# A hybrid decoder layer on one core: TensorE's order pinned slot by slot

## The chip, the cores and the metric

The kernel runs on one core of a Trainium2 chip. The metric is the device time of one execution in microseconds; lower is better. The median of the three runs shown of the kernel before is 1281.58 us.

## The reference, cut to what matters

One layer of a hybrid trunk for a prompt of 2048 positions and, beside it, 8 sequences of 4 new positions each, all with 1024 channels. `h = rmsnorm(x)` goes through one projection of 25 blocks of 128 columns. 13 of these blocks are shifted in time and feed an RWKV-7 recurrence of 8 heads of 64; 4 are its gate; 4 feed causal means over windows of 2, 4, 8 and 16 positions, and 4 are the gate of these.

```python
def _wkv_step(S, inp):
    r, w, k, v, kk, a = inp
    sa = jnp.einsum('bhvk,bhk->bhv', S, -kk)
    S = S * w[:, :, None, :] + sa[..., None] * (kk * a)[:, :, None, :] + v[..., None] * k[:, :, None, :]
    y = jnp.einsum('bhvk,bhk->bhv', S, r)
    return S, y
...
    out = jnp.concatenate([o_rwkv, o_pool], axis=-1) @ w_out.astype(f32)
    return x.astype(f32) + out, p_rwkv[:, -1], S_fin, u_ext[:, -POOL_BUF:]
```

The recurrence's output is normed per head, gated and joined with the gated means; an output projection of 1024 x 1024 and a last RMSNorm follow. The states after the last position are outputs too.

## The kernel before, in words

**Main work.** The prompt is cut into 4 groups of 512 positions. Every group has 25 projections (`proj`, L330): 8 chunks of 128 input channels, each with three products into one PSUM bank (L345 to L347: high part of the weights with the high and the low part of `x`, low part with the high). One such chunk is called a **slot** here. After each slot the generator yields, so a group has 200 slots and the four groups 800 (in the last group, which carries the 32 new positions too, a slot is two chunks of 272 columns). The output projection (`out_tile`, L1143) follows: 16 tiles of 16 slots each. While `x` of the first group arrives, `first_x` and `first_norm` (L238, L266) make its norm afterwards; for later groups `stats` and `prep_x` (L218, L280) prepare it in lane `x`.

**Side work.** Per group there are 4 head pairs, called **units** (`unit`, L522), each 48 slots long: the projections of r, k, window input, v and the two gates. When the projection of k has ended, VectorE and ScalarE shift it and make from it the blocks `abd` and `bk` and, for the key norms, a high and a low part `h_sq` and `l_sq` (L536 to L550, L471 to L475). The unit's recurrence is then done in chunks of 64 positions by side work:

- `decay` (L483): two products of the low-rank part of the block m = 12 (`lora_in` L378, `lora_out` L391), before the unit.
- `key_norms` (L502): the products `sq` and `bo` (L479, L480). The row `dS` goes to DRAM by ScalarE's queue (L513).
- `products` (L575): four steps of `pa` (L588), then, once the fold before has ended (`pend`), four steps of `pb` (L619).
- `solve` (L628): the blocks `Ab` go to DRAM by ScalarE's queue (`dA`, L637) and come back as `L` on SyncE's queue (L642). GpSimd then runs a substitution of 31 double operations (L654, L656) and three masks (L666, L668) as soon as `pb` is done. TensorE transposes its result (`xt`, L676) and does `q1` and `q2` (L695, L703).
- `fold` (L728): four times `z` (L733), copied into a block matrix by ScalarE and VectorE, and `f` (L741), added to `F` by VectorE.
- `pair_chain` (L763): eight dependent steps `ch` (L774), VectorE making the next state between them. `pair_back` (L803) norms the output in some 20 small VectorE operations and transposes it (`try`, L811).
- `values` and `pool_out` (L713, L859): one block of transposes `trv`, and one product `po`.

**What sets the order.** `run` (L461) calls `side()` after every slot; `side()` steps each lane's generator once. A number of `yield`s is a delay in slots. The compiler's list scheduler then orders every engine's instructions by priority and by when it thinks that they are ready. `tc.issue_after(ins)` adds an order edge: what the block traces on `ins`'s engine stands behind `ins` in the queue, without waiting for it to finish. In `side()` that instruction is the slot's last product (`mark[0]`). So a side product can't stand ahead of its slot, but can stand any number of slots behind it; and nothing holds the main products back. A unit starts only if fewer than two units are alive and lane `prod` is empty; until then it calls `side()` without main products.

Of the kernel before, what the change touches and what calls it, by code (L numbers as in the profile page):

```python
# [2 lines left out]

# [13 lines left out]
P = 128  # L17
# [43 lines left out]
def tile_trunk(ctx, tc, xT, xtok, xsT, xstok, par, w_in, wlora, pool_w, w_out, norm_f, st_shift, st_wkv, st_pool,  # L61
# [268 lines left out]
    def proj(g, m, xs):  # L330

        i = order.index((g, m))
        hi, lo = wts.pop(i)
        late_load = i + 2 < len(order) and order[i + 2][0]
        if not late_load:
            w_load(i + 2)
        last = g == NG - 1
        segs = []
        w = 272 if last else 512
        for s in range(2 if last else 1):  # L340
            pp = bank("pp", f"pp_{g}_{m}_{s}", 3) if i else bank("ch", "pp_first", 1)
            c = slice(s * w, (s + 1) * w)
            for kc in range(KC):
                xh, xl = xs[kc]
                PE.matmul(pp[:, :w], hi[:, kc, :], xh[:, c], start=(kc == 0), stop=False)  # L345
                PE.matmul(pp[:, :w], hi[:, kc, :], xl[:, c], start=False, stop=False)  # L346
                mark[0] = PE.matmul(pp[:, :w], lo[:, kc, :], xh[:, c], start=False, stop=(kc == KC - 1)).ins  # L347
                if s == 0 and kc == 2:
                    w_split(i + 1)
                    if late_load:  # L350
                        w_load(i + 2)
                if not last or kc % 2:
                    yield
            if g == 0 and m != 12:
                V.tensor_tensor(out=pp, in0=pp, in1=rb0[0], op=mult)
            if last:
                A.activation(spr[:, m, 16 * s:16 * s + 16], pp[:, 256:272], AF.Copy)
                segs.append((pp, 256 * s, 256))
            else:
                segs.append((pp, 0, G))  # L360
        return segs
# [44 lines left out]
            V.scalar_tensor_tensor(out=sg[:, a:a + n], in0=t1[:, a:a + n], scalar=1.0, in1=pp[:, :n], op0=add, op1=mult)  # L406
        return sg

    DH, DZ, DP, YQ = 6, 2, 4, 16

    def c3(ap):
        return ap.rearrange("p (c t) -> p c t", t=CH)
# [3 lines left out]
    rb0, low = [], []  # L416
    pend = [0]
    made = [None]
    chb = []
    lanes = {"prod": [], "solve": [], "fold": [], "chain": [], "x": [], "tail": []}  # L420
    late = []
# [23 lines left out]
    def drain(lane):  # L445
        while lanes[lane]:
            step(lane)

    def side():
        if not mark:  # L450
            return
        with tc.issue_after(mark[0]):
            step("solve")

            with tc.high_priority(0):
                step_late()
                step("prod")
                step("fold")
                step("chain")
# [42 lines left out]
    def key_norms(g, j, u, kk2, prod):  # L502

        nm = f"{g}_{j}"
        a = head_sums(kk2, f"sq_{nm}")
        for _ in range(DH + 2):
            yield
        sq = head_sums_mm(a, f"sq_{nm}")
        sqs = sb.tile([P, 512], F32, tag="tmp", name=f"sqs_{nm}", bufs=3)
        A.activation(sqs, sq, AF.Copy)  # L510
        for h in range(2):
            for b in range(2):
                nc.scalar.dma_start(u["dS"][b, h:h + 1],  # L513
                                    sqs[64 * h:64 * h + 1].rearrange("p (c b t) -> p b c t", b=2, t=32)[:, b])
        a = head_sums(prod, f"bo_{nm}")
        for _ in range(DH):
            yield
        bo = head_sums_mm(a, f"bo_{nm}")
        u["bv"] = sb.tile([P, 512], F32, tag="bv", name=f"bv_{nm}")
        A.activation(u["bv"], bo, AF.Copy)  # L520

    def unit(g, j, xs, nxs, lst, nst):  # L522
        nm = f"{g}_{j}"
        u = {}
        later((DZ if g else DZ + 7) if j == 0 else 1, decay(g, j, lst, u))
        r = shift(g, j, (yield from proj(g, j, xs)), "rps", 1)
        k = shift(g, 4 + j, (yield from proj(g, 4 + j, xs)), "kps", 1)
        while alive[0] >= 2 or lanes["prod"]:
            side()
        alive[0] += 1  # L530
        lam, cs, tha = u["lam"], u["cs"], u["tha"]
        kk2 = sb.tile([P, 512], F32, tag="tmp", name=f"kk2_{nm}", bufs=3)
        A.activation(kk2, k, AF.Square, scale=pr[:, KK + j:KK + j + 1])
        for h in range(2):
            q = slice(64 * h, 64 * h + 64)
            V.scalar_tensor_tensor(out=abd[q, :, q], in0=c3(k)[q], scalar=pr[q, KK + j:KK + j + 1],  # L536
                                   in1=lam[q, :, 0:CH], op0=mult, op1=mult)
        ab = sb.tile([P, 512], F32, tag="t1", name=f"ab_{nm}")
        A.activation(ab, tha, AF.Identity, scale=nkk[:, j:j + 1], bias=nkk[:, j:j + 1])
        V.tensor_tensor(out=cs, in0=k, in1=cs, op=mult)  # L540
        V.tensor_tensor(out=bk[:, :, 0:CH], in0=c3(cs), in1=c3(ab), op=mult)
        rd = sb.tile([P, NCH, CH], F32, tag="rd", name=f"rd_{nm}", bufs=1)
        V.tensor_tensor(out=rd, in0=c3(r), in1=lam[:, :, 1:], op=mult)
        A.activation(tha, tha, AF.Identity, scale=hka[:, j:j + 1], bias=oka[:, j:j + 1])
        V.tensor_tensor(out=bk[:, :, CH:2 * CH], in0=c3(cs), in1=c3(tha), op=mult)  # L545
        for h in range(2):
            q = slice(64 * h, 64 * h + 64)
            nc.sync.dma_start(rbd[q, :, h], rd[q])
        prod = sb.tile([P, 512], F32, tag="pd", name=f"prod_{nm}", bufs=1)
        V.scalar_tensor_tensor(out=c3(prod), in0=rd, scalar=pr[:, RK + j:RK + j + 1],  # L550
                               in1=bk[:, :, CH:2 * CH], op0=mult, op1=mult)
        dS = dr.tile([2, 2, NCH, 32], F32, tag="dS", name=f"dS_{nm}")
        u.update(rd=rd, dS=dS)
        lanes["prod"].append(products(g, j, u))
        kn = key_norms(g, j, u, kk2, prod)
        next(kn)
        late.append(kn)
        for m in SEQ[2:]:
            if m == 17:
                d = yield from pool_in(g, j, xs)  # L560
            elif m == 8:
                u["v"] = shift(g, 8 + j, (yield from proj(g, 8 + j, xs)), "kps", 1)
                later(8, values(g, j, u))
            elif m == 21:
                sg = gate(g, 21 + j, (yield from proj(g, 21 + j, xs)), "th0")
                later(DP, pool_out(g, j, d, sg))
            else:
                u["sg"] = gate(g, 13 + j, (yield from proj(g, 13 + j, xs)), "sg")
            if m == (SEQ[3] if SEQ[2] == 8 else 8):
                V.tensor_tensor(out=u["bv"], in0=u["bv"], in1=u["v"], op=mult)  # L570
            if m == SEQ[4] and j == NPAIR - 1 and g < NG - 1:
                drain("x")
                lanes["x"].append(prep_x(g + 1, nst, nxs, range(XB - KC, KC)))

    def products(g, j, u):  # L575

        nm = f"{g}_{j}"
        for _ in range(3):
            yield

        ka = sb.tile([P, NCH, P], F32, tag="ka", name=f"ka_{nm}")
# [30 lines left out]
        for b in range(4):  # L612
# [8 lines left out]
            A.activation(f, pb[64:128], AF.Copy)  # L621
            for h in range(2):
                A.activation(rb[64 * h:64 * h + 64, cr, :], pb[0:64, :, h, :], AF.Copy)
            yield
            yield
        u["made"] = True

    def solve(g, j, u):  # L628
# [5 lines left out]
        for h in range(2):  # L634
            for b in range(2):
                o = 64 * h + 32 * b
                nc.scalar.dma_start(dA[b, h].rearrange("c t i -> t c i"), Ab[o:o + 32, :, 32 * b:32 * b + 32])  # L637
        L = sb.tile([P, 32, 32], F32, tag="L", name=f"L_{nm}", bufs=1)
        a2 = sb.tile([P, 32], F32, tag="a2", name=f"a2_{nm}")
        for q in range(4):  # L640
            nc.sync.dma_start(a2[32 * q:32 * q + 32], dS.rearrange("b h c t -> (b h c) t"))
            nc.sync.dma_start(L[32 * q:32 * q + 32], dA.rearrange("b h c t i -> (b h c) t i"))  # L642
        for _ in range(6):
            yield
        V.tensor_scalar(out=a2, in0=a2, scalar1=L2_EPS, scalar2=None, op0=add)
        V.reciprocal(a2, a2)  # L646
# [39 lines left out]
        with tc.issue_after(made[0]):  # L686
            for h in range(2):
                o = 64 * h + 32
                V.transpose(T22[o:o + 32], tbd[o:o + 32, :, o:o + 32])
        yield  # L690
        q1 = [bank("mm", f"q1_{nm}_{h}", 2, (P, NCH, 32)) for h in range(2)]
        for c in range(NCH):
            for h in range(2):
# [2 lines left out]
        for h in range(2):  # L696
            o = 64 * h
            A.activation(qs[o:o + 32], q1[h][o:o + 32], AF.Copy)
        q2 = [bank("mm", f"q2_{nm}_{h}", 2, (P, NCH, 32)) for h in range(2)]
        for c in range(NCH):  # L700
            for h in range(2):
# [26 lines left out]
    def fold(g, j, u):  # L728

        def front(b):  # L730
            z = bank("pt", f"z_{g}_{j}_{b}", 2, (P, 2, P))
            for c in range(2):
                PE.matmul(z[:, c, :], tbd[:, 2 * b + c, :], u["rb"][:, 2 * b + c, :], start=True, stop=True)  # L733
            zb = zbd[b % 2]
# [3 lines left out]
        def back(b):  # L738
# [3 lines left out]
                          zbd[b % 2][:, c].rearrange("p h t -> p (h t)"), start=True, stop=True)  # L742
            d = u["fm"][b // 2][:, 2 * (b % 2):2 * (b % 2) + 2]
            V.tensor_tensor(out=d, in0=f, in1=d, op=add)  # L744
            u["folded"] += 2

        yield
        front(0)
        for b in range(4):
            yield  # L750
            if b < 3:
                front(b + 1)
            yield
            back(b)
        pend[0] = 0
        yield

# [45 lines left out]
    def pair_back(g, j, u, Y):  # L803
        nm = f"{g}_{j}"
        yn = Y.rearrange("p a h v -> p (a h) v")
        group_norm(yn, yn, P, 8, nm)
        for _ in range(5):
            yield
        tr = bank("pt", f"try_{nm}", 2)
        for i in range(4):  # L810
# [332 lines left out]
    def out_tile(o, res, dst, n, wo, nm):  # L1143
# [12 lines left out]
        for f in range(2):  # L1156
            pp = bank("pp", f"po_{nm}_{f}", 3)
            for c in range(8):
                wh, wl = wo[c, f]
                PE.matmul(pp[:m], hi[:, c, :m], wh, start=(c == 0), stop=False)  # L1160
                mark[0] = PE.matmul(pp[:m], hi[:, c, :m], wl, start=False, stop=(both and c == 7)).ins  # L1161
                if not both:
                    mark[0] = PE.matmul(pp[:n], lo[:, c, :n], wh, start=False, stop=(c == 7)).ins  # L1163
# [123 lines left out]
```

## Time and profile before

| | |
|---|---|
| runs shown, us | 1283.13, 1276.70, 1281.58 (median 1281.58) |
| the profiled execution's own time, us | 1273.72 |
| its span, first to last instruction, us | 1272.0 |
| TensorE matmuls busy | 1186.1 us, 93% |
| VectorE, ScalarE, GpSimd busy | 65%, 44%, 39% |
| mean granted TensorE clock | 0.972 |

Read it in this way: the profiled execution lies 7.9 us below the median. TensorE's busy time counts overlapping products once, so the rest of the span is time in which it had no product under way. Idle time of the other engines matters where TensorE waits for them.

### The profile page before, as it was taken

What the parts mean: (1) busy time and instruction counts of PE and PEld (TensorE: products, weight loads), DVE (VectorE), ACT (ScalarE), POOL (GpSimd) and SP (SyncE); (2) the same over time, 40 slices, a digit from 0 to 9 for tenths busy, and PEclk for the clock granted to TensorE, in tenths of its full rate; (3) what the DMA queues carried; (4) which work ended last, traced back from release to release, by engine and by line L of the source; (5) the groups of instructions that cost most, each with busy time, mean ns of one, the idle gap of its engine ahead of it and who ended that gap; (6) DMA issues with size and microseconds to landing.
All of it is one profiled execution on the core that took longest, in us unless ns stands there. A gap on an engine that the chain in (4) does not pass through costs nothing. (4 is left out here: it accounts for less than half of the span.)

```text
span 1272.0 us, 21094 instructions
## 1 busy us (share of the span) xinstructions
PE 1186.1 (93%) x7229; PEld 977.9 (77%) x7229; DVE 830.7 (65%) x2028; ACT 563.4 (44%) x1363; POOL 500.9 (39%) x1138
## 2 busy tenths in 40 slices
PE   7996999889989999999899899989999999999997
PEld 4765777677878788788687789889889877887685
DVE  6845767857566756866576767564656577745764
ACT  4563645444445444546353546453535453321112
POOL 6054728172343754818064708270808370000000
PEclk7997999999999999999999999999999999999999
DMA  7774555454566554546374556444444444433431
GB/s 248 236 245 138 204 184 192 155 187 153 142 208 173 169 144 144 175 150 205 116 201 140 148 154 184 131 149 126 137 130 140 121 147 151 149 112 99 131 110 66
DMA packets 153372, 200.18 MB, mean 157 GB/s; under 512 B 82480, under 2 KB 99120, under 8 KB 153264
## 3 DMA queue, kind: packets, MB, share of 16 engines
q1 hardware_dynamic: 109632, 104.90, 26.9%
q10 hardware_dynamic: 43632, 93.93, 23.6%
q8 instruction: 57, 0.93, 0.3%
q14 instruction: 51, 0.42, 0.1%
HBM read 139.39 MB, written 46.80 MB: 146 GB/s over the span
## 5 line engine op out<-in xcount | busy, mean ns | idle before, releaser
L345 PE MATMUL pp<-xh,wh 128*128 128x512 f32 (+1 forms) x992 | 366.3, 370 | 8.8 <-ACT xh L204 5.3
L346 PE MATMUL pp<-xl,wh 128*128 128x512 f32 (+1 forms) x992 | 363.4, 366 | 1.3 <-DVE xl L205 1.2
L347 PE MATMUL pp<-xh,wl 128*128 128x512 f32 (+1 forms) x992 | 362.4, 366 | 0.5 <-DVE wl L325 0.5
L345 PEld LDWEIGHTS pp<-xh,wh 128*128 128x128 f32 x992 | 189.4, 191 | 34.5 <-ACT xh L204 6.3
L346 PEld LDWEIGHTS pp<-xl,wh 128*128 128x128 f32 x992 | 189.5, 191 | 24.9 <-DVE xl L205 2.4
L347 PEld LDWEIGHTS pp<-xh,wl 128*128 128x128 f32 x992 | 189.1, 191 | 24.1 <-DVE wl L325 1.8
L654 POOL TENSOR_TENSOR Xt<-X,L 128x60 f32<-128x60 f32 (+24 forms) x496 | 186.3, 376 | 38.9
L656 POOL TENSOR_TENSOR X<-X,Xt 128x60 f32<-128x60 f32 (+24 forms) x496 | 183.0, 369 | 38.9
L649 POOL TENSOR_TENSOR X<-dmask,a 128x256 f32<-128x256 bf16 x16 | 10.8, 675 | 288.8 <-DVE a L646 288.8
L647 POOL TENSOR_TENSOR L<-L,a 128x1024 f32<-128x1024 f32 x16 | 31.8, 1990 | 170.4 <-DMA L<-dA 170.4
L774 PEld LDWEIGHTS ch<-SV,F 128*128 128x128 f32 x512 | 74.5, 191 | 18.6 <-ACT Y L778 8.5
L774 PE MATMUL ch<-SV,F 128*128 128x64 f32 x512 | 79.5, 266 | 2.2 <-DVE F L744 0.9
L741 PE MATMUL f<-zbd,ka 128*128 128x256 f32 x256 | 68.2, 387 | 0.6 <-DVE zbd L736 0.3
L1160 PE MATMUL po_o<-woh,oh_o 128*128 128x512 f32 x160 | 66.8, 418 | 0.0
L776 DVE TENSOR_TENSOR SV<-ch,lc 64x128 f32<-64x128 f32 x112 | 33.0, 295 | 51.2 <-PE ch L774 46.6
L1163 PE MATMUL po_o<-woh,ol_o 128*128 128x512 f32 x160 | 65.1, 407 | 0.2 <-DVE ol_o L1151 0.2
L1161 PE MATMUL po_o<-wol,oh_o 128*128 128x512 f32 x160 | 65.1, 407 | 0.0
L588 PE MATMUL pa<-bk,abd 128*128 128x192 f32 x256 | 54.4, 358 | 10.2 <-DVE bk L545 6.3
L736 DVE COPY zbd<-z 64x256 f32<-64x256 f32 x64 | 27.1, 427 | 53.8 <-ACT zbd L735 52.7
L778 ACT ACTIVATE Y<-ch 64x128 f32<-64x128 f32 x128 | 34.2, 267 | 61.6 <-DVE SV L776 55.7
L744 DVE TENSOR_TENSOR F<-f,F 128x512 f32<-128x512 f32 x64 | 44.2, 690 | 25.8 <-PE f L741 22.4
L588 PEld LDWEIGHTS pa<-bk,abd 128*128 128x128 f32 x256 | 47.8, 211 | 15.4 <-issue 6.6
(447 smaller groups left out, 2330.1 us busy)
## 6 DMA issues: line engine op xcount, KB each, us to landing
wh<-wh ACTq DMA_DIRECT2D x75, 512.0 KB
wl<-wl ACTq DMA_DIRECT2D x75, 512.0 KB
wr<-in_w_in ACTq DMA_DIRECT2D x25, 512.0 KB
wh<-wh SPq DMA_DIRECT2D x25, 512.0 KB
wl<-wl SPq DMA_DIRECT2D x25, 512.0 KB
xr<-in_xT SPq DMA_DIRECT2D x32, 256.0 KB
L<-dA SPq DMA_DIRECT2D x64, 128.0 KB
oi<-o_d SPq DMA_DIRECT2D x16, 512.0 KB
```

Of the source, the lines that this page charges most:

```text
L345: PE.matmul(pp[:, :w], hi[:, kc, :], xh[:, c], start=(kc == 0), stop=False)
L346: PE.matmul(pp[:, :w], hi[:, kc, :], xl[:, c], start=False, stop=False)
L347: mark[0] = PE.matmul(pp[:, :w], lo[:, kc, :], xh[:, c], start=False, stop=(kc == KC - 1)).ins
L588: PE.matmul(pa[:, c, :], abd[:, 2 * b + c, :], bk[:, 2 * b + c, :], start=True, stop=True)
L654: GP.tensor_tensor(out=tm, in0=X[:, :n, i:i + 1].broadcast_to([P, n, w]), in1=L[:, i + 1:, i].unsqueeze(1).broadcast_to([P, n, w]), op=mult)
L656: done = GP.tensor_tensor(out=X[:, :n, i + 1:], in0=X[:, :n, i + 1:], in1=tm, op=add).ins
L741: PE.matmul(f[:, c].rearrange("p h t -> p (h t)"), u["ka"][:, 2 * b + c, :], zbd[b % 2][:, c].rearrange("p h t -> p (h t)"), start=True, s ...
L744: V.tensor_tensor(out=d, in0=f, in1=d, op=add)
L774: PE.matmul(ch[:, h, :], fm[cc // 4][:, cc % 4, h, :], sv[cc // 4][:, cc % 4, h, :], start=True, stop=True)
L1160: PE.matmul(pp[:m], hi[:, c, :m], wh, start=(c == 0), stop=False)
L1161: mark[0] = PE.matmul(pp[:m], hi[:, c, :m], wl, start=False, stop=(both and c == 7)).ins
L1163: mark[0] = PE.matmul(pp[:n], lo[:, c, :n], wh, start=False, stop=(c == 7)).ins
```

## The change

TensorE's queue gets a second kind of edge: the first main product of a slot is put behind the last side product that the `side()` before it traced (`behind`, `lastpe`). With the old edge the order is then main products, side products, main products, with each side product that is the last of its step bound to its slot. The delays in slots are changed with it: `DZ` 2 to 5 (decay of a group's first unit), `YQ` 16 to 9 and the wait at the start of `solve` 6 to 8, values 8 to 12, `products` 3 to 9 ahead of `pa` and 2 to 3 between `pb` steps, two slots more around `q1` and `q2`, three slots instead of one or two from `z` to `f`, the chain's leave (`folded`) two slots behind `f`, `try` 5 to 8. `z` moves from the PSUM tag `pt` to `mm`. The writes of `dS` and `dA` move from ScalarE's queue to SyncE's.

```diff
@@ proj
-                PE.matmul(pp[:, :w], hi[:, kc, :], xh[:, c], start=(kc == 0), stop=False)
+                with behind():
+                    PE.matmul(pp[:, :w], hi[:, kc, :], xh[:, c], start=(kc == 0), stop=False)
...
-    DH, DZ, DP, YQ = 6, 2, 4, 16
+    DH, DZ, DP, YQ = 6, 5, 4, 9
...
+    lastpe = []
...
+    def behind():
+
+        return tc.issue_after(lastpe.pop()) if lastpe else nullcontext()
+
     def side():
         if not mark:
             return
+        block = nc.cur_bb.bb.instructions
+        at = len(block)
+        side_steps()
+        pe = [i for i in block[at:] if i.engine == mark[0].engine]
+        if pe:
+            lastpe[:] = pe[-1:]
+
+    def side_steps():
         with tc.issue_after(mark[0]):
             step("solve")
...
@@ key_norms
-                nc.scalar.dma_start(u["dS"][b, h:h + 1],
+                nc.sync.dma_start(u["dS"][b, h:h + 1],
@@ unit
-                later(8, values(g, j, u))
+                later(12, values(g, j, u))
@@ products
-        for _ in range(3):
+        for _ in range(9):
             yield
...
-            yield
-            yield
+            for _ in range(3):
+                yield
         u["made"] = True
@@ solve
-                nc.scalar.dma_start(dA[b, h].rearrange("c t i -> t c i"), Ab[o:o + 32, :, 32 * b:32 * b + 32])
+                nc.sync.dma_start(dA[b, h].rearrange("c t i -> t c i"), Ab[o:o + 32, :, 32 * b:32 * b + 32])
...
-        for _ in range(6):
+        for _ in range(8):
             yield
...
-        yield
+        for _ in range(2):
+            yield
         q1 = [bank("mm", f"q1_{nm}_{h}", 2, (P, NCH, 32)) for h in range(2)]
...
+        for _ in range(2):
+            yield
         q2 = [bank("mm", f"q2_{nm}_{h}", 2, (P, NCH, 32)) for h in range(2)]
@@ fold
-            z = bank("pt", f"z_{g}_{j}_{b}", 2, (P, 2, P))
+            z = bank("mm", f"z_{g}_{j}_{b}", 2, (P, 2, P))
...
-            u["folded"] += 2
-
-        yield
+
+        for _ in range(2):
+            yield
         front(0)
         for b in range(4):
             yield
             if b < 3:
                 front(b + 1)
             yield
+            yield
             back(b)
+            yield
+            yield
+            u["folded"] += 2
@@ pair_back
-        for _ in range(5):
+        for _ in range(8):
             yield
@@ out_tile
-                PE.matmul(pp[:m], hi[:, c, :m], wh, start=(c == 0), stop=False)
+                with behind():
+                    PE.matmul(pp[:m], hi[:, c, :m], wh, start=(c == 0), stop=False)
```

## Rows read from the trace of the kernel before

**Rows 1.** The page, parts 1 and 2: TensorE's busy time, and its granted clock.

```profile
PE 1186.1 (93%) x7229; PEld 977.9 (77%) x7229; DVE 830.7 (65%) x2028; ACT 563.4 (44%) x1363; POOL 500.9 (39%) x1138
PEclk7997999999999999999999999999999999999999
```

**Rows 2.** Busy time by stretch: length, each engine busy (instructions), PEclk, DMA share, GB/s.

```profile
106.00:273.00 167.00, 157.27 (x935) 126.47 (x936) 118.11 (x257) 82.58 (x186) 77.10 (x173) 0.96 0.53 172
273.00:302.00 29.00, 22.45 (x86) 16.64 (x85) 23.50 (x49) 11.88 (x23) 17.63 (x34) 0.88 0.48 159
302.00:517.00 215.00, 207.88 (x1267) 169.74 (x1266) 141.18 (x327) 102.88 (x256) 98.81 (x216) 1.00 0.55 164
517.00:757.00 240.00, 228.83 (x1363) 186.37 (x1363) 158.14 (x386) 118.31 (x291) 112.16 (x255) 0.99 0.53 157
757.00:1010.00 253.00, 237.53 (x1904) 224.94 (x1903) 156.33 (x396) 117.86 (x337) 119.18 (x273) 0.99 0.48 140
```

**Rows 3.** Waits of TensorE: us in total, times, longest us.

```profile
PE try L811 <- DVE Y L801: 13.3, 13, 2.1
PE xt L676 <- POOL X L656: 11.8, 1, 11.8
PE sq L479 <- ACT h_sq L472: 7.9, 3, 3.3
PE pa L588 <- DVE bk L545: 6.3, 2, 3.2
PE try L811 <- DVE carry L375: 4.2, 1, 4.2
```

**Rows 4.** Timeline of TensorE: main products behind a chain step, then undisturbed.

```profile
710.52 0.48 PE L347 MATMUL pp<-xh,wl 128*128 128x512 f32 x1
710.84 0.39 PE L345 MATMUL pp<-xh,wh 128*128 128x512 f32 x1
711.07 0.39 PE L346 MATMUL pp<-xl,wh 128*128 128x512 f32 x1
711.76 0.40 PE L346 MATMUL pp<-xl,wh 128*128 128x512 f32 x1
```

**Rows 5.** Timelines of ScalarE and VectorE at the start of unit 6 (units counted from 0).

```profile
422.04 0.69 ACT L370 ACTIVATE t<-pp,om 128x512 f32<-128x512 f32 x1 [5.00 <-PE pp L347]
...
423.76 1.57 DVE L536 SCALAR_TENSOR_TENSOR abd<-kps,pr,lam 64x512 f32<-64x512 f32 x2
...
427.44 0.79 DVE L474 TENSOR_TENSOR l_sq<-kk,h_sq 128x512 fp32r<-128x512 f32 x1
```

**Rows 6.** Timelines of ScalarE, VectorE and GpSimd at the start of unit 11.

```profile
717.44 0.69 ACT L370 ACTIVATE t<-pp,om 128x512 f32<-128x512 f32 x1 [2.97 <-PE pp L347]
...
722.36 4.58 DVE L536 SCALAR_TENSOR_TENSOR abd<-kps,pr,lam 64x512 f32<-64x512 f32 x2
...
729.76 0.68 DVE L474 TENSOR_TENSOR l_sq<-kk,h_sq 128x512 fp32r<-128x512 f32 x1
...
722.14 2.56 POOL L666 TENSOR_TENSOR F<-F,mkr 64x512 f32<-64x512 f32 x2
724.67 1.72 POOL L668 TENSOR_TENSOR rb<-rb,mkr 128x512 f32<-128x512 f32 x1
```

**Rows 7.** Timelines of TensorE and VectorE at the start of the second group.

```profile
294.38 0.73 PE L345 MATMUL pp<-xh,wh 128*128 128x512 f32 x2 [2.88 <-ACT xh L204]
...
301.56 0.69 DVE L386 TENSOR_TENSOR sw<-lth,sw 64x512 fp32r<-64x512 f32 x1
...
303.93 0.39 PE L394 MATMUL z<-sw,lwh 128*128 128x512 f32 x1
```

**Rows 8.** Timeline of VectorE at the start of the third group.

```profile
531.84 0.75 DVE L371 SCALAR_TENSOR_TENSOR tmp<-pp,pr,t 128x511 f32<-128x511 f32 x1
...
535.96 0.69 DVE L386 TENSOR_TENSOR sw<-lth,sw 64x512 fp32r<-64x512 f32 x1
```

**Rows 9.** The lines of the moved writes: issue time in ns min/median/max, first and last us.

```profile
L637 ACTq DMA_DIRECT2D dA<-Ab x64: 309/326/674, 63.2 to 998.8; - x64
...
L513 ACTq DMA_DIRECT2D dS<-sqs x64: 606/607/1207, 59.8 to 993.6; - x64
```

More of the change, by code (lines that the diff above doesn't have):

```diff
@@ L1 @@
 import math
-from contextlib import ExitStack
+from contextlib import ExitStack, nullcontext
 import concourse.bass as bass
```

## The prediction

> **What bounds the kernel now.** I read the page first: TensorE has a product under way in 1186.1 of 1272.0 us, every other engine 65% at most [rows 1]. So TensorE's queue sets the time, and a change of its order can move two things: the 86 us in which it has nothing under way, and the time in which its clock is granted at half. Next I read the busy time by stretch [rows 2], each length less its TensorE time: 9.7 us idle in the first group behind 106 us, 6.6 at the change to the second group, 7.1 in the second, 11.2 in the third, 15.5 in the fourth. That is 50 us in 904, about 1 us for each 18: what is to be won from 106 us on is small. The granted clock is 0.96, 0.88, 1.00, 0.99 and 0.99 of 2.4 GHz there. A mean of 0.96 means 8% of the stretch at 1.2 GHz, which costs half of that time; over the five stretches it is 6.7 + 3.5 + 0 + 2.4 + 2.5 = 15 us if TensorE was busy meanwhile. Then the waits of TensorE [rows 3]: `try` 13.3 + 4.2 us, `xt` once 11.8, `sq` 7.9, `pa` 6.3. No other wait of a side product adds up to as much as 2 us from 106 us on.
>
> How long is a slot? Undisturbed, the same line's products stand 711.76 - 711.07 = 0.69 us apart, 0.23 each; the first one behind a chain step takes 0.32 [rows 4]. A group's 200 slots last 215 us in the second group [rows 2], 1.07 us each, side products included.
>
> **The change, part by part.** The work on TensorE stays the same, so I sum its idle time.
>
> *Slots, counted from the yields.* Now `solve` takes 51 steps of lane `solve` for each unit. Then it takes 49, but `pb` waits for the fold before, and `pb` (12), masks, `YQ` and `fold` (23) close a ring of 51 steps again. As 50 slots are there for each unit, four `side()` calls in each group run without main products: 16 in all. They cost nothing by themselves, as the main products only come later; they take slack from `try`. Steps with a side product are 389 now and 434 then. At 0.09 us for each return [rows 4] that would be +4 us if every step were a block of its own today; the order now cuts some steps up, so I take **+1** (bounds -5, +4).
>
> *Key norms, the largest term.* `sq` keeps its 8 slots behind the end of the unit's k product, but now the next slot can't start without it. 8 x 0.69 = 5.5 us of main products, and some 0.5 us of a `try` in half of the units, lie ahead of it. What it needs is `l_sq`. In a quiet unit that ends at 427.44 + 0.79 = 428.23, 6.2 us after ScalarE began to read the k product at 422.04 [rows 5]: 0.2 to 0.7 us late, and I take 0.8 with the waits on semaphores. In a disturbed one it ends at 730.44, 13.0 us behind 717.44 [rows 6], 7 us late, of which some 1.5 belongs to a `try` that ran into it: 5.5. What disturbed it is GpSimd: the two `abd` operations took 4.58 us instead of 1.57 just while the masks ran from 722.14 to 726.39 [rows 5, 6]. Fourteen units count (the first two lie under the wait for `xt`). Bounds: none disturbed, 14 x 0.8 = 11 us; all, 14 x 5.5 = 77. I take 4 disturbed, near the low end, because the masks last 4.3 us of a unit's 60: 10 x 0.8 + 4 x 5.5 = 30 us. `pa`, two slots later, then finds its inputs there. Against 7.9 + 6.3 = 14.2 now [rows 3]: **+16** (bounds -3, +63).
>
> The Trainium skill, GPSIMD Engine Reference, section Specifications, says that GpSimd shares its SBUF interfaces with VectorE and contends with VectorE instructions that have two SBUF inputs; `abd` has two, and rows 6 agree. By this rule alone every unit whose masks fall into its first 7 us would be a disturbed one; that is the second rival.
>
> *Decay.* At the second and third change of group the decay product stands 6 slots behind the end of m = 12: 4.1 us of main products and two blocks of `pb` at about 0.44. It needs `sw`, which ends at 536.65, 4.8 us after VectorE began to read m = 12 at 531.84, itself about 1 us behind the product [rows 8]. So it is 0.8 us late if VectorE is free and up to 2 if `group_norm` runs between: 1.5 twice, **+3** (bounds 0, +12).
>
> *First change of group.* `x` of the second group is ready only at 294.4 us [rows 7]. Counted in order, TensorE had done 226 slots when the first decay product started at 303.93, 2 us behind `sw`; by the new edges it has done 214 then. The 12 slots x 0.69 = 8.3 us are still to be done, less one `pb` block and one `try` that now come later too: **+7** (bounds 0, +12).
>
> *`try`.* In order it stands 9 to 15 slots behind the chain's last step today; by the new count 8 to 11 slots and three `pb` blocks, 8 + 2 to 11 + 2 in time. Nothing much is gained in distance, but the spread goes: of 17.5 us [rows 3] I take **-7** (bounds -13, +5).
>
> *`xt`, first unit.* GpSimd's substitution sets this wait [rows 3], and `xt` stands at slot 80 instead of 79. At the start TensorE will stop for the norm of the first group, which today's order fills with later slots; the wait at `xt` then swallows that. The write on another queue may bring `L` 2 us earlier: **-2** (bounds -10, +8). Later units have 41 steps from `dA` to `xt` instead of 46, 5 us less; `xt` mostly shares its step with a `pa` that carries the edge, so it can slip: 0.
>
> *Moved writes.* 64 x 0.33 + 64 x 0.61 = 60 us of issuing leave ScalarE [rows 9], which is 44% busy [rows 1], and go to SyncE's queue. Behind a write that waits for `Ab` or `sqs` stand there the loads of `L` and `a2`, which need it anyhow, and loads of `x` and fills of `F`, which have slots to spare. 0; if the cover goes, some 2 us per unit reach `xt`, which is within the range.
>
> *`z`, `q1`, `q2`, chain, `po`, output tiles.* Their inputs are ready within two or three slots today and get more: 0. *Clock:* the longest of today's waits stand beside the stretches at half clock; a few more of them, **+2** (bounds -12, +10).
>
> Sum: 1 + 16 + 3 + 7 - 7 - 2 + 2 = **+20 us**. The profiled execution took 1273.72 us, 7.9 below the median; 1293.7 for one like it, and 1281.6 + 20 = **1302 us** for the median.
>
> **The rivals.**
>
> *The bound slots are late enough: faster.* If TensorE meets no late input, `sq` and `pa` give 11 of their 14 us back, `try` 13, the clock 8 and `xt` 4, while the changes of group still cost 4: -32, 1250 us. For it: all new delays are near where the products stand in today's order, and the waits that remain are 2 us and less [rows 3]. Against it: `sq` was not moved, and a wait can no longer be filled with a later slot. It decides at 6 us: `l_sq` must end by then, measured from the read of the k product [rows 5].
>
> *Every start of a unit is hit: much slower.* The new ring ties `made`, and with it the masks, to the start of the next unit: in two of four units of a group their step comes one behind it, in the others up to five ahead, and GpSimd's lag puts them later. If 10 of 14 units are disturbed, `sq` waits 10 x 5.5 + 4 x 0.8 = 58 us, +44 instead of +16; with the changes of group, +10, and the clock, +4: +58, 1340 us.
>
> *The waits change places.* `sq` +5, first change of group +5, `try` -9: about 1283 us. The edges bind only the last product of a step, and within one projection the slots were in order already.
>
> **How the numbers follow.** This kernel's runs differ so that 0.5% (6.4 us) can just be told from no change. My forecast has 0.40, "every start is hit" 0.12, "the waits change places" 0.18, "late enough" 0.30. So slower 0.52, same 0.18, faster 0.30. The range runs from the price of the faster rival, 1250, to near that of the much slower one, 1335; half of each of these two lies outside, about 0.2. The likeliest sign has 0.52, little more than half; its own range is 1288 to 1335.
>
> **What would show it.** In the changed kernel's waits of TensorE, `sq` behind `h_sq` or `l_sq` should be the first line with about 30 us, `pa` near none, `try` about 10, decay behind `sw` some 3 with longest 2. In the timeline of the second group's start the first decay product should stand behind 214 slots. The mask operations should overlap long `abd` operations in about 4 units. The forecast is wrong if `sq` waits under 10 us in all, or if TensorE's idle time falls below 80 us.

## The result, and the profile after

The changed kernel takes 1294.28 us (median of four runs, 1291.87 to 1296.71), the kernel before 1280.53 us (four runs, 1276.70 to 1283.13). The ratio is 1.0115, with a 95% interval of 1.0090 to 1.0139: slower by 14 us, where 20 were forecast. The profiled executions differ by 23.0 us (spans 1272.0 and 1295.0), because the one of before lies low among its runs and the one of after high. Three of e5's twelve executions below were in a slower state and are left out of its figures.

TensorE's busy time and granted clock after, from parts 1 and 2 of the page; they answer to [rows 1]:

```profile
PE 1192.0 (92%) x7229; PEld 989.9 (76%) x7229; DVE 820.5 (63%) x2028; ACT 567.1 (44%) x1363; POOL 476.2 (37%) x1138
...
PEclk7898988898999998899999998999999979998899
```

Idle is 1295.0 - 1192.0 = 103.0 us, against 85.9: +17.1. Busy is +5.9. The mean granted clock fell from 0.972 to 0.947. A mean of 0.947 means 2 x 0.053 x 1295 = 137 us at 1.2 GHz, against 71 before.

The busy time by stretch after, columns as in [rows 2] (the stretches follow the same work, so their ends are later):

```profile
106.00:273.00 167.00, 144.46 (x818) 115.92 (x818) 106.33 (x235) 74.35 (x164) 61.50 (x145) 0.89 0.50 159
273.00:310.00 37.00, 30.46 (x132) 23.25 (x131) 21.51 (x41) 11.64 (x27) 25.62 (x63) 0.86 0.49 153
310.00:525.00 215.00, 206.09 (x1257) 170.19 (x1257) 137.99 (x338) 108.48 (x262) 87.22 (x205) 0.97 0.55 159
525.00:765.00 240.00, 225.92 (x1337) 186.50 (x1337) 153.42 (x383) 118.26 (x288) 111.11 (x267) 0.98 0.53 157
765.00:1020.00 255.00, 244.75 (x2002) 231.40 (x2001) 162.40 (x416) 125.23 (x350) 110.31 (x269) 0.98 0.52 148
```

In the same first 167 us TensorE begins 818 products instead of 935, at a mean clock of 0.89 instead of 0.96 [rows 2]. The idle time is 22.5 us there (9.7 before), 6.5 at the change of group, 8.9, 14.1 and 10.3 later: in the fourth group it even fell (15.5 before).

The waits of TensorE after, columns as in [rows 3]:

```profile
PE sq L493 <- ACT h_sq L486: 12.5, 8, 6.0
PE sq L494 <- DVE l_sq L488: 9.2, 9, 2.0
PE xt L690 <- POOL X L670: 6.9, 1, 6.9
...
PE try L832 <- DVE kps L374: 6.2, 1, 6.2
PE try L832 <- DVE Y L822: 5.2, 3, 3.8
...
PE sq L493 <- ACT tbd L694: 4.5, 4, 2.1
PE bo L493 <- ACT X L713: 4.0, 8, 0.5
...
PE z L395 <- DVE sw L387: 2.1, 3, 0.8
...
PE try L832 <- ACT t L371: 0.9, 1, 0.9
...
PE pa L602 <- DVE ka L604: 0.5, 1, 0.5
```

`sq` is first with 12.5 + 9.2 + 4.5 = 26.2 us (about 30 were expected), `pa` has 0.5, `try` 6.2 + 5.2 + 0.9 = 12.3, decay behind `sw` 2.1 in three waits.

### The profile page after: what moved, and what is told of

It is laid out like the page before. It is cut to its first block, busy times and chain, and to the rows that moved or that the text cites. A ratio compares the mean times of both kernels' runs of the same rounds, so it can differ in the third digit from the quotient of the medians.

```text
span 1295.0 us, 21148 instructions
## 1 busy us (share of the span) xinstructions
PE 1192.0 (92%) x7229; PEld 989.9 (76%) x7229; DVE 820.5 (63%) x2028; ACT 567.1 (44%) x1363; POOL 476.2 (37%) x1138
## 4 chain that ended last, share of the span: by engine, by line
PE 68%; DVE 16%; DMA 5%; ACT 5%; POOL 3%; issue 2%; SPq 1%; ACTq 0%; DVEq 0%; POOLq 0%
PE pp L346 10%; PE pp L347 10%; PE pp L348 10%; PE po_o L1182 5%; PE po_o L1183 4%; PE po_o L1185 4%; PE f L758 4%; PE ch L795 3%; PE pa L602 3%; PE z L750 2%; DVE abd L550 1%; POOL Xt L668 1%; DMA xr<-in_xT 1%; POOL X L670 1%; PE pb L633 1%
## 5 line engine op out<-in xcount | busy, mean ns | idle before, releaser
L346 PE MATMUL pp<-xh,wh 128*128 128x512 f32 (+1 forms) x992 | 403.1, 406 | 6.5 <-ACT xh L204 6.5
L347 PE MATMUL pp<-xl,wh 128*128 128x512 f32 (+1 forms) x992 | 358.9, 362 | 1.8 <-DVE xl L205 1.7
L348 PE MATMUL pp<-xh,wl 128*128 128x512 f32 (+1 forms) x992 | 358.4, 362 | 0.0
L346 PEld LDWEIGHTS pp<-xh,wh 128*128 128x128 f32 x992 | 193.8, 195 | 25.7 <-ACT xh L204 8.0
L347 PEld LDWEIGHTS pp<-xl,wh 128*128 128x128 f32 x992 | 194.3, 196 | 22.0 <-DVE xl L205 3.9
L668 POOL TENSOR_TENSOR Xt<-X,L 128x60 f32<-128x60 f32 (+24 forms) x496 | 177.0, 357 | 38.8
L670 POOL TENSOR_TENSOR X<-X,Xt 128x60 f32<-128x60 f32 (+24 forms) x496 | 168.7, 340 | 38.8
L795 PEld LDWEIGHTS ch<-SV,F 128*128 128x128 f32 x512 | 76.4, 195 | 18.5 <-issue 5.2
L795 PE MATMUL ch<-SV,F 128*128 128x64 f32 x512 | 73.9, 267 | 6.4 <-DVE F L761 3.9
L680 POOL TENSOR_TENSOR F<-F,mkr 64x512 f32<-64x512 f32 x32 | 44.3, 1390 | 61.9 <-ACT F L635 60.5
L758 PEld LDWEIGHTS f<-zbd,ka 128*128 128x128 f32 x256 | 49.1, 196 | 10.5 <-issue 1.2
```

Of the source, the lines that this page charges most:

```text
L668: GP.tensor_tensor(out=tm, in0=X[:, :n, i:i + 1].broadcast_to([P, n, w]), in1=L[:, i + 1:, i].unsqueeze(1).broadcast_to([P, n, w]), op=mult)
L670: done = GP.tensor_tensor(out=X[:, :n, i + 1:], in0=X[:, :n, i + 1:], in1=tm, op=add).ins
L680: GP.tensor_tensor(out=t, in0=t, in1=mkr[0:64].unsqueeze(1).broadcast_to([64, 8, CH]), op=mult)
L758: PE.matmul(f[:, c].rearrange("p h t -> p (h t)"), u["ka"][:, 2 * b + c, :], zbd[b % 2][:, c].rearrange("p h t -> p (h t)"), start=True, s ...
L795: PE.matmul(ch[:, h, :], fm[cc // 4][:, cc % 4, h, :], sv[cc // 4][:, cc % 4, h, :], start=True, stop=True)
```

## The experiments

Twelve kernels. Ratios are to runs of the kernel before on the same chip, with 95% intervals; 1% is 12.8 us. Differences between two kernels below are differences of these ratios. Idle is the profiled span less TensorE's busy time, clock that execution's mean; both are of one execution, which for e2, e5 and e7 is the fastest of the kernel's runs.

| kernel | median us | ratio | idle us | clock |
|---|---|---|---|---|
| changed kernel | 1294.28 | 1.0115 [1.0090, 1.0139] | 103.0 | 0.947 |
| e1: without the edge | 1254.32 | 0.9817 [0.9788, 0.9845] | 75.2 | 0.971 |
| e2: before, edge alone | 1450.78 | 1.1346 [1.1314, 1.1378] | 210.7 | 0.925 |
| e3: edge from slot 225 | 1273.22 | 0.9961 [0.9941, 0.9982] | 88.5 | 0.957 |
| e4: sq two slots later | 1288.15 | 1.0081 [1.0052, 1.0110] | 104.4 | 0.961 |
| e5: e1, writes back | 1272.70 | 0.9951 [0.9924, 0.9978] | 85.2 | 0.973 |
| e6: e1, z back | 1253.27 | 0.9804 [0.9776, 0.9832] | 73.2 | 0.970 |
| e7: late products not bound | 1268.46 | 0.9930 [0.9902, 0.9958] | 88.5 | 0.970 |
| e8: before, writes and z moved | 1271.63 | 0.9953 [0.9927, 0.9979] | 80.7 | 0.965 |
| e9: edge, writes back | 1300.98 | 1.0169 [1.0135, 1.0202] | 106.0 | 0.950 |
| e10: e7, no edge at changes | 1258.02 | 0.9824 [0.9791, 0.9856] | 83.7 | 0.966 |
| e11: key norms not bound | 1275.68 | 0.9964 [0.9937, 0.9992] | 92.1 | 0.960 |
| e12: e1, old back delays | 1276.90 | 0.9988 [0.9966, 1.0011] | 88.5 | 0.960 |

**e1: the edge away, all else kept.**

```diff
     def behind():
-        return tc.issue_after(lastpe.pop()) if lastpe else nullcontext()
+        return nullcontext()
```

> The changed kernel with all its delays and its moved writes, but without the new edge: main products no longer wait for the side() before them. Theory A (the edge does two things of opposite sign: it packs the side products into whole blocks, which takes some 20 us of switching out of TensorE's busy time, and it keeps TensorE from filling a wait, which costs 17 us of idle time and about 65 us more at half clock): without it TensorE's idle time falls from 103 to 75 to 90 us, the mean granted clock rises from 0.947 to 0.965 or more, the busy time at full clock rises again, and the time is that of the kernel before, 1274 to 1287 us. Theory B (the loss comes from the new delays and from SyncE's queue, not from the edge): it stays at 1290 to 1300 us with sq, try and xt still the first waits.

Neither theory foresaw 1254.3 us. The edge costs 3.0% (38 us), and the delays and moves without it are worth 1.8% (23 us) against the kernel before: the change has one good and one bad half.

**e2: the edge alone, on the kernel before** (the hunks `behind`, `lastpe`, `side_steps` of the change and nothing else).

> The kernel before with the new edge alone, all delays and queues as they were. pa stands 4 slots behind the end of the k product here (2.8 us of main products), while bk ended 5.5 to 22 us behind it in the kernel before. Theory A (the edge makes TensorE wait for each late input, so the new delays are what makes it bearable): pa waits 3 to 7 us in most of 16 units, 40 to 100 us in all, the clock falls below 0.94, and the time is 1320 to 1400 us. Theory B (the delays are what cost, the edge is free or gains): 1265 to 1285 us.

Theory A, and more: +13.5%. Its first two waits of TensorE:

```profile
PE pa L602 <- DVE bk L559: 69.8, 14, 10.1
PE try L825 <- DVE Y L815: 36.4, 10, 8.9
```

With the old delays `pa` is bound 4 slots behind k, where its input can't be ready, and `try` follows. The free order hides most of this: in the kernel before, with the same delays, `pa` waits 6.3 us for `bk` [rows 3].

**e3: the edge only from slot 225 on.**

```diff
-    def behind():
+    def behind(i=99):
-        return tc.issue_after(lastpe.pop()) if lastpe else nullcontext()
+        return tc.issue_after(lastpe.pop()) if lastpe and i >= 28 else nullcontext()
...
-                with behind():
+                with behind(i):
```

> The changed kernel with the edge left out in the first 224 slots (the first group and the start of the second), everything else as in the changed kernel. Theory A1 (the loss is made where inputs are late by many slots, at the start of the first group and at the first change of group: in the two traces the changed kernel is 23 us behind at slot 208 and 19 us behind at slot 800): 15 to 25 us come back, 1270 to 1280 us, and the waits of sq (6.0 us), try (6.2 and 3.8 us) before 300 us are gone or filled. Theory A2 (the loss is spread over the units' starts, sq in each): under 8 us come back, 1287 to 1294 us.

1.54% come back, 20 us: theory A1. The other 18 of the edge's 38 us are lost in the later three groups and the output. But with the edge kept there e3 is no slower than the kernel before (0.9961): set against that kernel, the whole loss is made before slot 225, and behind it the new delays give back what the edge costs.

**e4: `sq` two slots later, `bo` in its place.**

```diff
-        for _ in range(DH + 2):
+        for _ in range(DH + 4):
...
-        for _ in range(DH):
+        for _ in range(DH - 2):
             yield
         bo = head_sums_mm(a, f"bo_{nm}")
```

> The changed kernel with sq two slots later behind the end of the k product (10 instead of 8), bo where it was (its delay behind sq is 4 instead of 6 slots). Theory A2 (sq's late inputs set the loss): two slots are 1.4 us, so the nine waits of sq up to 2.5 us go nearly away; of 26 us of sq's waits 10 to 13 us remain, the first unit's 6.0 us among them, and with some clock the time is 1274 to 1284 us. Rival (the wait moves on to the next product of the same block, pa or bo, or is filled elsewhere): bo's or pa's waits rise by about as much as sq's fall and the time is 1289 to 1297 us.

Between the two, 1288.2 us, and no clear difference from the changed kernel (the intervals overlap). The waits moved on, to `pa`, which now shares the slot:

```profile
PE pa L602 <- DVE ka L604: 12.9, 13, 2.2
...
PE sq L493 <- ACT h_sq L486: 3.4, 1, 3.4
```

TensorE's idle time did not fall (104.4 us); what fell, from the one profiled execution to the other, is the time at half clock, from 137 to 2 x 0.039 x 1286 = 100 us.

**e11 and e7: products with late inputs are not bound.** In e11 `sq` and `bo`, in e7 `xt`, decay and `try` too, are left out when `side` picks the product that the next slot must follow.

```diff
-        pe = [i for i in block[at:] if i.engine == mark[0].engine]
+        pe = [i for i in block[at:] if i.engine == mark[0].engine and id(i) not in free]
...
-        sq = head_sums_mm(a, f"sq_{nm}")
+        with loose():
+            sq = head_sums_mm(a, f"sq_{nm}")
```

(`loose` puts what is traced inside it into `free`.)

> The changed kernel with its edge, but sq and bo alone not bound to their slot; xt, decay and try are. Theory S (sq, the prediction's largest term, carries most of what the late products cost, 26 us in e7): 1266 to 1277 us. Rival (try, xt and decay carry as much as sq): 1279 to 1288 us.

> The changed kernel with its edge, but sq, bo, xt, decay and try are never the product that the next slot stands behind; all other side products still are. Theory W (the edge costs its 40 us through the late inputs of these few products, and the idle time and the half clock that follow them): idle time of TensorE 60 to 75 us, mean clock 0.968 or more, 1240 to 1258 us, so at or below the kernel without any edge. Rival O (any fixed order costs, because the many small waits of z, q, f, ch and pa can't be filled either): 1268 to 1288 us.

e11 gives back 1.51% (19 us), theory S: the key norms, `sq` and `bo` together, are half of what the edge costs. e7 adds 0.34%, within the intervals. Theory W fails: by its time e7 lies in rival O's range, its idle time of 88.5 us misses the 60 to 75, and it stays 14 us above e1. Rival O's reason, small waits spread about, doesn't hold either, as e10 shows.

**e10: e7, and no edge where a group begins.**

```diff
-    def behind():
+    def behind(i=99):
+        if i < 4 or i in (24, 25, 26, 49, 50, 51, 74, 75, 76):
+            return nullcontext()
```

> The kernel of e7 (edge, but sq, bo, xt, decay and try not bound; 1268.5 us) with the edge left out, besides, in the first four projections and in the last one of a group and the first two of the next. Theory X (what e7 still loses against the kernel without any edge, 14 us, is lost where x of a group arrives chunk by chunk: in the traces e7 is 8.3 us behind at slot 208, and takes 5, 5 and 10 us more over the first 8 slots of the three later groups): 1242 to 1257 us, at or below the kernel without the edge, because the packing of the other blocks stays. Rival O (the rest is spread over many small waits): 1262 to 1272 us.

1258.0 us, theory X but for the last microsecond of its range: 1.06% (14 us; 10 by the two medians) come back, and what remains is no different from e1. The start of the fourth group shows one place of it. TensorE's timeline in e7:

```profile
761.66 0.66 PE L809 MATMUL ch<-SV,F 128*128 128x64 f32 x4 [1.00 <-ACT Y L813]
...
762.75 0.29 PE L348 MATMUL pp<-xh,wl 128*128 128x272 f32 x1
764.95 0.39 PE L346 MATMUL pp<-xh,wh 128*128 128x272 f32 x1 [1.92 <-ACT xh L204]
765.81 0.60 PE L347 MATMUL pp<-xl,wh 128*128 128x272 f32 x1 [0.47 <-DVE xl L205]
```

and in e1:

```profile
758.98 0.54 PE L346 MATMUL pp<-xh,wh 128*128 128x272 f32 x3
...
761.98 0.52 PE L346 MATMUL pp<-xh,wh 128*128 128x272 f32 x2 [0.34 <-ACT xh L204]
```

`x` comes chunk by chunk. Bound, TensorE waits 1.92 us for the next chunk's high part and 0.47 for its low part; free, it takes other main products whose inputs are there (three and two of the first form in a row; the view doesn't name their chunk or projection), and waits 0.34. This is some 2 us of the 14; the other starts were not read one by one.

**e9 and e5: the writes of `dS` and `dA` back on ScalarE's queue**, with the edge and without.

```diff
-                nc.sync.dma_start(u["dS"][b, h:h + 1],
+                nc.scalar.dma_start(u["dS"][b, h:h + 1],
...
-                nc.sync.dma_start(dA[b, h].rearrange("c t i -> t c i"), Ab[o:o + 32, :, 32 * b:32 * b + 32])
+                nc.scalar.dma_start(dA[b, h].rearrange("c t i -> t c i"), Ab[o:o + 32, :, 32 * b:32 * b + 32])
```

> The changed kernel (1294.3 us) with its edge and all its delays, but with the writes of dS and dA back on ScalarE's queue. TensorE's order is fixed here, so a difference is what the queue itself does, and not another order chosen by the compiler. Theory N (the move is worth nothing, as the prediction said: the 60 us of issuing lie beside other work): 1288 to 1300 us. Rival Q (ScalarE's h_sq, copies of pa and of tbd stand behind these issues and are late by them, as the 17 to 20 us between the two kernels without the edge suggest): sq, pa, xt and q wait longer and the time is 1305 to 1320 us.

> The changed kernel without the edge (1254.3 us) and, besides, with the writes of dS and dA back on ScalarE's queue. Theory D (the new delays bring the 23 us by which that kernel lies under the kernel before): 1250 to 1259 us. Rival Q (the 60 us of issuing taken off ScalarE bring them: h_sq, the copies of Ab, xt and q come earlier): 1268 to 1279 us.

The move saves 0.54% (7 us) with the edge, between the two theories and barely clear of noise (the intervals just touch), and 1.34% (17 us) without: rival Q there. In e9's waits of TensorE `pa` stands with

```profile
PE pa L602 <- DVE ka L604: 6.5, 7, 1.7
```

against 0.5 in the changed kernel. In e5, of the view of the `dA` write's line (L651), what waited behind it on its engine:

```profile
who waited for it (us, times):
  ACT zbd L752: 7.6, 5
  ACT bv L534: 2.4, 2
```

and TensorE's first wait:

```profile
PE xt L690 <- POOL X L670: 16.8, 2, 13.8
```

ScalarE's copies of the fold stand behind the issues, and `xt` waits 16.8 us (7.6 in e1), `pa` 10.9 (1.0 in e1). That the one makes the other is not shown. Without the edge the compiler also gives TensorE another order, so not all 17 us need be the queue's.

**e6: `z` back in the tag `pt`**, without the edge.

```diff
-            z = bank("mm", f"z_{g}_{j}_{b}", 2, (P, 2, P))
+            z = bank("pt", f"z_{g}_{j}_{b}", 2, (P, 2, P))
```

> The changed kernel without the edge (1254.3 us) and, besides, with z back in the tag pt. Theory D (the new delays bring the 23 us): 1250 to 1259 us. Rival Z (z no longer takes a bank of pt from pa, pb, f and try, and that brings them): 1266 to 1279 us.

No difference from e1: rival Z falls.

**e8: the kernel before with the writes and `z` moved** (the three hunks above, the other way round).

> The kernel before with only the writes of dS and dA on SyncE's queue and z in the tag mm; old delays, no edge. Theory D (the delays bring the gain of the kernel without the edge): 1270 to 1285 us. Rivals Q and Z (queue and bank bring it): 1252 to 1264 us.

-0.47%: theory D by its range. But with e5 (-0.49% for the delays with `z` moved) and e1 (-1.83% for both), neither the delays nor the moved writes are worth much without the other.

**e12: e1 with the back half of the delays as before.**

```diff
-        for _ in range(2):
-            yield
+        yield
         q1 = [bank("mm", f"q1_{nm}_{h}", 2, (P, NCH, 32)) for h in range(2)]
...
             yield
-            yield
             back(b)
-            yield
-            yield
-            u["folded"] += 2
...
-        for _ in range(8):
+        for _ in range(5):
             yield
         tr = bank("pt", f"try_{nm}", 2)
```

(and one slot less ahead of `front(0)`, two less ahead of `q2`, `folded` raised in `back` again.)

> The changed kernel without the edge (1254.3 us), with the delays of the unit's back half as in the kernel before: one yield ahead of q1, none between q1 and q2, z to f one slot, the chain free right behind f, try 5 slots behind. The delays of the front half (pa 9 slots, pb 3, solve 8, YQ 9, DZ 5, values 12), the writes on SyncE and z in mm stay. Theory back (these later steps bring the 17 us that the delays are worth beside the moved writes: try waits 18.1 us with the old delays and 11.5 with the new, and q, ch and z less too): 1264 to 1276 us. Theory front (pa behind sq instead of ahead of it brings them): 1250 to 1259 us.

1276.9 us, just above theory back's range, but not for its reason. `try` waits less than in e1:

```profile
PE xt L690 <- POOL X L670: 21.7, 3, 10.9
PE try L825 <- DVE Y L815: 7.4, 8, 1.6
```

(11.5 us in e1), while `xt` waits 21.7 us for GpSimd. With `YQ` at 9 it seems to be the longer fold that keeps `xt` far enough behind the substitution, so that the delays work as one set; no run shows this by itself. Which of them brings the 17 us that separate e1 from e8, where all are old, stays open.

## Why the prediction was right, and where it was not

**The sum held by parts that did not all hold.** By its own steps it was +17 of idle time (16 + 3 + 7 - 7 - 2), +1 for switching and +2 for the clock. The two profiles give +17.1 us of idle time and +5.9 of busy time. That 14 us came where 20 were forecast is in part luck: the busy time, the place of the loss and the key norms (further below) came out otherwise than the sum had them.

*Busy time.* Two other kernels split the +5.9, e1 without the edge and e7 with it. From part 1 of their pages:

```profile
PE 1177.3 (94%) x7229; PEld 970.2 (77%) x7229; DVE 826.6 (66%) x2028; ACT 566.2 (45%) x1363; POOL 486.6 (39%) x1138
...
PE 1173.5 (93%) x7229; PEld 971.0 (77%) x7229; DVE 819.0 (65%) x2028; ACT 565.7 (45%) x1363; POOL 479.3 (38%) x1138
```

Both have nearly the clock of the kernel before (0.971 and 0.970 against 0.972), which is busy 1186.1 us. So 8.8 us go with the new delays and moves, without any edge, and the blocks that the edge makes bring at most 3.8 more. The step on slots had **+1 (bounds -5, +4)** for the switching; -12.6 stands in its place, and most of it isn't the order in blocks. The changed kernel, bound like e7 but for the late products, has 0.947 and is busy 1192.0, 18.5 us more than e7; read as the price of the clock, that stands where **+2 (bounds -12, +10)** did. The two executions are extremes of their kernels (the others were granted 0.952 to 0.955 and 0.963 to 0.967). Against the mean of the kernel before, about 0.970, the mean of the changed kernel's four, 0.952, gives in proportion an estimate of some 14 us, still above the bound. Both terms left their bounds, in opposite directions.

One place of the saving is the group of `q1` and `q2` in the view by line, before and after:

```profile
L703 PE MATMUL q<-tbd,X 32*32 32x32 f32 x512 | 21.1, 192 | 0.0
L695 PE MATMUL q<-X,Ab 32*32 32x32 f32 x512 | 18.0, 192 | 2.1 <-DVE X L689 1.5 <-ACT bv L520 0.5
...
L720 PE MATMUL q<-tbd,X 32*32 32x32 f32 x512 | 14.8, 195 | 1.6 <-ACT tbd L724 1.6
L710 PE MATMUL q<-X,Ab 32*32 32x32 f32 x512 | 13.5, 192 | 1.1 <-ACT X L713 1.0
```

The same 1024 products have nearly the same mean each: they now overlap more. In e1 they are busy 17.0 + 15.4 us, so here too the larger part comes without the edge. I had priced the return to the main products alone.

*Place.* The largest term lay at the units' starts, twelve of its fourteen behind slot 225. But by e3 the net loss lies ahead of slot 225, and the two traces agree: 23 us behind at slot 208, 19 at slot 800 (e3's expectation). Idle time rose by 12.8 us and the clock fell from 0.96 to 0.89 in the stretch from 106 to 273 us, where the steps had little but **-2** at `xt` and the key norms of two units.

**The clock**: the step assumed a few more waits like those of before. But while TensorE waits at a bound product it has nothing else to do. By stretch around one wait of `try` in the first group, columns as in [rows 2]:

```profile
240.00:243.40 3.40, 0.01 (x1) 0.00 (x0) 3.23 (x9) 1.37 (x3) 1.25 (x1) 0.99 0.69 184
243.40:250.20 6.80, 4.00 (x12) 3.36 (x13) 6.74 (x12) 3.73 (x7) 1.26 (x1) 0.50 0.54 190
250.20:262.00 11.80, 11.35 (x58) 9.32 (x57) 9.52 (x19) 5.50 (x15) 0.00 (x0) 1.00 0.42 157
```

TensorE is idle for 6.2 us and then works another 4 us at 1.2 GHz. The price of a wait is the wait and what follows it. The Trainium skill, TensorE: Matmul & The Clock Gate, Terms, puts the penalty at the throttled time times the lost share of the clock. For the 61 us by which the changed kernel stands longer at half clock than e7 (137 against 2 x 0.030 x 1262 = 76) that is an estimate of 30 us. The trace has less, 18.5 in busy time. The window above shows one reason: of its 6.8 us at half clock TensorE was busy 4.0.

**Key norms, +16**: right in gross size, not in the difference. After, `sq` and `pa` wait 26.7 us together against the 30 of the step. Before, they waited 18.7 us and not 14.2, as the step left out

```profile
PE pa L588 <- DVE nwt_g L55: 1.8, 1, 1.8
PE pa L588 <- DVE ka L590: 1.8, 2, 1.5
...
PE sq L480 <- DVE l_sq L474: 0.9, 1, 0.9
```

so the rise is 8 us. `bo`, which the step had at nothing, waits 4.9 us (0.3 before). The 19 us of e11 are `sq`, `bo` and the clock behind them, measured against the changed kernel and not against the one before. The make-up was wrong too. The quiet units were to wait 0.8 us, the disturbed ones 5.5. Three units have a long `abd` under the masks (5, 9 and 15; four were assumed), and they wait 2.0 to 2.2 us. In 9, and for 1.3 of the 2.0 us in 5, the release named is a copy of `xt`, ScalarE's L694, which stands in the same slot; only in unit 15 is nearly all of it `l_sq`. VectorE and GpSimd in unit 9:

```profile
629.43 2.42 DVE L550 SCALAR_TENSOR_TENSOR abd<-kps,pr,lam 64x512 f32<-64x512 f32 x2
...
626.76 2.55 POOL L680 TENSOR_TENSOR F<-F,mkr 64x512 f32<-64x512 f32 x2
629.27 1.27 POOL L682 TENSOR_TENSOR rb<-rb,mkr 128x512 f32<-128x512 f32 x1
```

The quiet units 6, 7, 10 and 11 wait as long, 1.7 to 2.6 us. VectorE and TensorE in unit 6:

```profile
439.50 0.75 DVE L834 SCALAR_TENSOR_TENSOR o<-try,pr,bv 128x512 f32<-128x512 f32 x1 [1.80 <-PE try L832]
440.28 1.80 DVE L836 SCALAR_TENSOR_TENSOR og<-o,pr,sg 128x512 f32<-128x512 f32 x1
442.00 0.74 DVE L372 SCALAR_TENSOR_TENSOR kps<-pp,pr,t 128x511 f32<-128x511 f32 x1
...
445.96 0.50 PE L493 MATMUL sq<-h_sq,bonr 128*128 128x512 f32 x1 [0.93 <-ACT h_sq L486]
447.24 0.50 PE L494 MATMUL sq<-l_sq,bonr 128*128 128x512 f32 x1 [0.78 <-DVE l_sq L488]
```

The new count of slots puts `try` into the very slot in which k ends (slot 320 here), so VectorE reads k only after the two operations that `try` releases. I had charged `try` its time on TensorE, not what VectorE does for it. And the first unit waits 6.0 + 0.5 us for `sq`, as the prediction allowed, out of the wait at `xt`, which fell from 11.8 to 6.9. That `try` does this is read from the trace; no run moved it alone with the edge in place.

**Changes of group, +7 and +3**: the slots came as counted, the cause is only in part the edge. The first decay product of the second group starts at 316.63 us behind 214 slots, 0.77 us late for `sw`; counted in main products, slots 200 to 225 take 36.7 us instead of 30.0 us. By the same count e1 takes some 34, so part of the 7 is there without the edge. The later two decays wait 1.3 us together. e10 prices the starts of all four groups together at 14 us, and the clearest case, `x` arriving by chunks in the later groups, was not named.

**`try`, -7, and `xt`, -2**: 17.5 to 12.3 us and 11.8 to 6.9, both within their bounds. One wait of 6.2 us makes half of the 12.3 of `try`, though, in the window above; the step looked for many short ones.

**Moved writes, 0: wrong.** The step said that 60 us of issuing leave an engine that is 44% busy. They leave its queue too, where in e5 copies of the fold stood behind them: 7 us with the edge, 17 without. **`z`, `q1`, `q2`, chain, 0:** `z` holds (e6). The later steps from `q1` to `try` do not: without the edge, putting them back costs 1.71% (22 us, e12 against e1). With the edge they were not tried.

**The rivals.** "Late enough" priced a TensorE that meets no late input at 1250 us; e1, which may fill its waits, takes 1254. Its condition, `l_sq` within 6 us of the read of k, is met or nearly met in the first units of the later groups (5.9 to 6.3 us, in the fourth from the read of its second part), and their `sq` doesn't wait; most others take 7 us and more. "Every start of a unit is hit" would need ten disturbed units; there are three. "The waits change places" had 1283 us; the rise of 8 us of `sq` and `pa` is nearer to its +5 than to +16, but its time is missed by 11 us.

**A better version.** e1 (0.9817) and e6 (0.9804) beat both kernels: keep the delays and the moved writes and leave the edge out.

## What to carry to other kernels

Here an order fixed by hand brought at most 4 us by packing, while a late input behind it cost the wait and, after one of 6.2 us, a stretch at half clock too; bind the products whose inputs are early, and leave free those behind a busy engine and those at a stage's start, where inputs arrive piece by piece. Count for a moved step what other engines do for it, not only its own product, and price a DMA issue by what stands behind it in its queue. When a change has two halves, run each alone: the total hid a gain of 23 us and a loss of 38.

## What the runs showed of the hardware

Idle time and clock are two prices. The profiled execution of e4 is idle as long as the changed kernel's (104.4 and 103.0 us) but granted 0.961 instead of 0.947, and 9 us of span lie between them. These are single executions: by all runs the two kernels are not clearly apart. Why the clock differs was not tried.

Issues on a compute engine's queue are not small here: by where the same 128 writes are issued, the time without the edge differs by 17 us (e5 against e1), TensorE's changed order included. The Trainium skill, DMA: Bandwidth & Descriptors, section Issuing engines are not separate DMA queues, says that issuing from several engines saves only the sequencer's time, usually small beside the transfer. The trace agrees on what is saved (the issues, 60 us of them [rows 9]); no run compares an issue with its transfer, but here the saving is not small in its effect.
